# Four adaLN vectors move from TensorE to VectorE, and the later query projections are spread over six heads

## The chip, the cores and the metric

The kernel runs on one core of a Trainium2 chip. The metric is device time in microseconds (us) for one execution. The engines are PE (TensorE, matrix products; PEld is its weight load), DVE (VectorE), ACT (ScalarE), POOL (GpSimd) and SP (the queue that issues all DMA loads here). Each engine works through its own queue in order; a semaphore wait at the head of a queue holds everything behind it.

## The reference, cut to what matters

Two layers of a diffusion trunk over 512 latent tokens of width 1024, with 256 context tokens. Each layer begins with `adaln_params`: six vectors (shift, scale and gate, twice) that come from one condition vector.

```python
def adaln_params(cond, w, bias):
    m = jax.nn.silu(cond) @ w + bias            # w: 1024 x 6144, one row vector at a time
    return jnp.split(m[..., None, :], N_MOD, axis=-1)
...
sh1, sc1, g1, sh2, sc2, g2 = adaln_params(c, mod_w[i], mod_b[i])
h = modulate(rms_norm(x, norm_g[i, 0]), sh1, sc1)
y = attention_mixers(h, ...)  or  fourier_mix(h) @ w_f
x = x + g1 * rms_norm(y, norm_g[i, 1])
h = modulate(rms_norm(x, norm_g[i, 2]), sh2, sc2)
x = x + g2 * rms_norm(conv_ffn(h, ...), norm_g[i, 3])
```

Layer 0 mixes with attention: eight heads of 128, four global (A, heads 0 to 3, all 768 keys, rms norm on q and k) and four with a window (B, heads 4 to 7, the context and up to three blocks of 128 keys). Layer 1 mixes with a Fourier transform. What matters here are the vectors of layer 0 number 2 to 5: g1, sh2, sc2 and g2. Each is a product of a vector of 1024 with a 1024 x 1024 matrix of 4 MB. None of them is needed before the output projection's norm, right after attention; number 5 is first needed at the end of the first FFN.

## The kernel before, in words

All values are fp32. A product is done as three products of fp32r parts (`mm3`, lines 90 to 92): high x high, high x low, low x high. `split` (line 113) makes the parts: ACT casts the high part, DVE (or POOL) subtracts it for the low part. Weights come as 1 MB pieces into a ring of three buffers named `raw` (line 122); SP issues the loads in the order in which they are written, and a load waits until the buffer three loads earlier has been read. So a slow reader of one piece holds up the pieces behind it.

The order on each engine follows the order in which the code is written, moved about by the framework's scheduler from its own estimate of when operands are ready; the code steers it with generators that are advanced (`pump`) by a number of steps at given places.

Up to the attention heads the stages are:

- The start (line 47 on): shift and scale of layer 0 are made by channel tile on PE (`M0` to `M7`, function `mod_tile`, tiles `misc`, `modc`, `derc`), the inputs are modulated (`md_t`, `hh`, `hl`), and keys and values of two groups are accumulated.
- The early projections: groups `kb`, `vb`, `qa`, eight blocks of 48 products of 256 columns into `mm`. Their weights are loads `in_w_in`. Between them DVE and POOL do norm and rotation of keys and queries (`roped`, tiles `K`, `yT`, `sq`, `kst`, `qst`).
- The heads: for each head and each of four query blocks, scores `S` on PE, maximum on DVE (line 854), exponential on ACT, sum and reciprocal on DVE, scaling of `P` on POOL (line 870). One head later `pv` transposes `P` (`PT`, line 786), splits it (`th`, `tl`) and multiplies it with the values into `O`.
- The remaining query projections (heads 2 to 7: six blocks of 48 products into `gm`) are the generator `rest`, with eight steps for a block: ten steps before head 0 and the others beside heads 0 to 3, as the table `FILL` says, two entries for a query block.
- The four late vectors of layer 0 are the generator `gem0` (`gemv_pe`): sixteen pieces `in_mod_p` of 1 MB, four small products each (line 405), advanced by `FILL` beside heads 4 to 7; then eight transposes (line 412).
- The output projection's first tiles (`out_first`, 24 products of 512 columns twice and 24 of 256, into `gm` and `S`) beside the last head. Results of the first heads are kept in the queries' place (`kept`) and split into `hh`, `hl` when the projections are done with them.

The six vectors of layer 1 are made in the first FFN by `gemv_jobs`: for a vector, four pieces `in_mod_r`; of each, DVE multiplies two 128 x 1024 tiles by a column of the condition and adds them to a sum `gacc` (lines 376 and 379); then PE sums over partitions (line 384), ACT copies, PE transposes twice (line 390), DVE adds the bias. The FFN advances it 35 steps; a vector takes five.

Of the kernel before, what the change touches and what calls it, by code (L numbers as in the profile page):

```python
# [10 lines left out]
F32 = mybir.dt.float32  # L11
# [4 lines left out]
ALU = mybir.AluOpType  # L16
# [18 lines left out]
# what is traced where: how far work of one kind runs ahead of another kind's  # L35
# [6 lines left out]
# products that keep the PE's clock up: at the start, before the first sums' use, before the second FFN  # L42
# [3 lines left out]
# the start, in the order in which the loads arrive: M, shift and scale of a channel tile; W, its key and value  # L46
# weights; F, its products with a half of the latents or the context; X, B, R, what the norms need
START = ("M0 W0 X0 M1 B0 W1 F00 X1 F10 M2 W2 M3 F01 F11 F20 W3 F21 M4 R2 F30 F31 F02 W4 F12 F22 F32 M5 W5 F40 "
         "F41 M6 F42 W6 F50 F52 W7 F60 M7 F62 F51 F61 F70 F71 F72")
# how much of other work goes with each half block of a head's tokens  # L50
FILL = [[1, 0, 1, 2, 3, 2, 1, 2],
# [7 lines left out]

# columns of the packed parameter array  # L60
C_C, C_CC, C_MB, C_NG, C_CW, C_CB = 0, 8, 16, 112, 176, 440
C_SINK, C_ALL = 528, 532
# columns of the packed constants
# [4 lines left out]
def kernel(ctx: ExitStack, tc: tile.TileContext, a):  # L68
# [25 lines left out]
    # issued after another one on the same engine  # L94
# [4 lines left out]
    # work that must not be issued ahead of the last instruction traced before a fence on its engine  # L99
# [61 lines left out]
    # products that keep the PE's clock up where it would have to wait  # L161
# [4 lines left out]
    # sums over channels: four column tiles of the PE hold a quarter of the tokens each  # L166
# [5 lines left out]
    # 1 / sqrt(sum / D + eps)  # L172
# [10 lines left out]
    # the same where only the time until the end counts: sums on all partitions at once  # L183
# [14 lines left out]
    # one quarter of the tokens per quadrant of partitions: side by side, then to all partitions  # L198
# [12 lines left out]
    # h = x * am * R + bm for several channel tiles, shared out over the engines  # L211
# [15 lines left out]
    # squares of y: summed over channel tiles by GpSimd, the last one by the PE  # L227
    class YStat:
# [8 lines left out]
        def add(self, pps, src, hs):  # L237
# [9 lines left out]
            # the halves of the last one share a tile where they come one after the other  # L247
# [26 lines left out]
    # x += gate * rms_norm(y) for one channel tile  # L274
# [11 lines left out]
    # x += gate * rms_norm(y); then the next sub-layer's modulated input  # L286
# [20 lines left out]
    # the same, but what follows gets the input x * am only: the token's factor is applied after the products  # L307
    # over channels, and the shift is added there
    class Plain:
        # sums of squares go where the first and the last tile of y are done with  # L310
# [32 lines left out]
        # the factors: tokens on partitions, or on all partitions  # L343
# [23 lines left out]
    # adaLN off the critical path: products and sums on DVE, the sum over partitions on the PE  # L367
    def gemv_jobs(jobs, pps):
        for l, v in jobs:
            acc = mk(cp, [P, D], F32, "gacc", 1)  # L370
            for kk in range(4):
                w = raw([P, 2, D], a["mod_r"][v, kk])
# [25 lines left out]
    # the same on the PE: four column tiles take a quarter of the columns each  # L398
    def gemv_pe(pps):
        for j in range(2):  # L400
            ps = mk(pps, [P, T], F32, "gm", 1)
            for k in range(KC):
                w = raw([P, 2048], a["mod_p"][j, k])
                for q in range(4):
                    PE.matmul(ps[32 * q:32 * q + 32, :], lhsT=spad[:, k, :], rhs=w[:, q * T:(q + 1) * T],  # L405
                              start=k == 0, stop=k == KC - 1)
                yield
            rs = mk(cp, [P, T], F32, "sq", 2)
            S.copy(out=rs, in_=ps)
            tp = mk(pps, [P, T], F32, "gm", 1)  # L410
            for b in range(4):
                PE.transpose(out=tp[:, b * P:(b + 1) * P], in_=rs[:, b * P:(b + 1) * P], identity=ident)
            V.tensor_tensor(out=mods[:, 0, 2 * j + 2:2 * j + 4, :].rearrange("p v k -> p (v k)").rearrange(
                                "p (j b) -> p j b", b=4),
                            in0=tp.rearrange("p (b j r) -> p j b r", b=4, r=32)[:, :, :, 0],
                            in1=cols[:, C_MB + 16 * j + 16:C_MB + 16 * j + 32].rearrange("p (j b) -> p j b", b=4),
                            op=ALU.add)
            for v in (2 * j + 2, 2 * j + 3):
                derive(0, v)
            yield  # L420

# [4 lines left out]
    # output projection's weights for two channel tiles  # L426
    def out_weights(u, xp):
        r = raw([P, KC, 256], a["w_out"][u])
        ws = []
        for i in range(2):  # L430
            wh, wl = (xp.pair if u >= 2 else wpair)([P, KC, P])
            split(wh, wl, r[:, :, i * P:(i + 1) * P])
            ws.append([(wh[:, k, :], wl[:, k, :]) for k in range(KC)])
        return ws

        # ------------------------------------------------------------ attention
    with ExitStack() as es:
        ap = es.enter_context(tc.tile_pool(name="ap", bufs=1, reuse_waits="tile"))
        Q = yT.rearrange("p a b -> p (a b)").rearrange("p (t d) -> p t d", d=D)
# [302 lines left out]
        with ExitStack() as e2:  # L742
# [79 lines left out]
            for head in range(8):  # L822
# [64 lines left out]
                if head == 3:  # L887
                    pump(rest, 1000)
# [547 lines left out]
```

## Time and profile before

| | us |
|---|---|
| runs: median (lowest to highest of 3) | 1177.17 (1176.93 to 1181.68) |
| span of the profiled execution | 1176.5 |
| PE busy | 1134.0 (96%) |
| DVE busy | 751.6 (64%) |
| ACT busy | 512.2 (44%) |
| POOL busy | 201.1 (17%) |
| read from HBM | 141.98 MB |

The page gives no time of its own for the profiled execution beside its span; the span lies 0.7 us below the median of the runs. Stages by the span's clock: the start to 74 us, early projections to 120 us, heads to about 262 us, the rest of head 7 with the first output products to 279 us, output projection to about 340 us, first FFN to about 685 us, then the Fourier mixer and the second FFN. Busy times are shares of a span with very different stages; a stage has to be read by itself. PE's matmul records overlap, so that "busy" there means that no gap lies between records.

### The profile page before, as it was taken

Reading aid. Unit: us, or ns where it says so; the run is one execution under the profiler, and the core shown is the slowest. Engines: PE = TensorE matmul, PEld = TensorE weight load, DVE = VectorE, ACT = ScalarE, POOL = GpSimd, SP = SyncE. Lnnn points to the kernel's source line nnn. Section 1 sums busy time; section 2 is a strip of 40 time slices with the busy share of each in tenths; the row PEclk is TensorE's granted clock in tenths of the full one; section 3 lists DMA queues with packets and bytes.
Section 4 is the critical chain, followed back from the end, with each engine's and each line's share of the span. In section 5 each row is a group of like instructions: output and inputs, shape, how many; then the busy total and the mean of one; then the engine's idle time right before and its main releaser. Section 6 shows DMA issues by size and latency. Waiting matters only on the chain.

```text
span 1176.5 us, 17135 instructions
## 1 busy us (share of the span) xinstructions
PE 1134.0 (96%) x6878; PEld 946.1 (80%) x6878; DVE 751.6 (64%) x1215; ACT 512.2 (44%) x887; POOL 201.1 (17%) x213
## 2 busy tenths in 40 slices
PE   7999999999999999999999998988999999999995
PEld 4689898679898877777878998877788888888895
DVE  4673777675779685756665568988966532255555
ACT  3332356566554434322444445646644332234342
POOL 1132534222320000000000153663000000000013
PEclk9999999999999999999999999998999999999998
DMA  9432110874115353666622301621233222332112
GB/s 371 187 127 72 37 36 7 298 306 152 65 43 209 108 208 110 237 238 225 233 90 56 116 11 35 210 81 60 72 108 103 73 84 99 108 108 72 54 55 72
DMA packets 27127, 145.18 MB, mean 123 GB/s; under 512 B 2724, under 2 KB 7460, under 8 KB 14120
## 3 DMA queue, kind: packets, MB, share of 16 engines
q1 hardware_dynamic: 27048, 144.09, 35.0%
q8 instruction: 54, 0.88, 0.3%
q14 instruction: 25, 0.20, 0.1%
HBM read 141.98 MB, written 2.10 MB: 122 GB/s over the span
## 4 chain that ended last, share of the span: by engine, by line
PE 84%; DVE 11%; DMA 1%; ACT 1%; issue 1%; POOL 1%; SPq 0%; DVEq 0%; ACTq 0%; POOLq 0%
PE mm L90 24%; PE mm L92 23%; PE mm L91 23%; DVE md_t L278 2%; PE PT L786 2%; PE gm L405 1%; DVE hl L333 1%; PE O L90 1%; DVE wl L113 1%; DVE xT L280 1%; PE S L90 1%; PE O L91 1%; PE O L92 1%; PE S L92 1%; DMA xT<-in_xT 1%
## 5 line engine op out<-in xcount | busy, mean ns | idle before, releaser
L113 DVE TENSOR_TENSOR wl<-raw,wh 128x1024 fp32r<-128x1024 f32 (+1 forms) x139 | 167.6, 1210 | 207.8 <-ACT wh L113 207.5
L90 PE MATMUL mm<-hh,wh 128*128 128x512 f32 (+2 forms) x728 | 276.1, 379 | 0.0
L92 PE MATMUL mm<-hh,wl 128*128 128x512 f32 (+2 forms) x728 | 275.7, 379 | 0.0
L91 PE MATMUL mm<-hl,wh 128*128 128x512 f32 (+2 forms) x728 | 275.4, 378 | 0.0
L113 ACT CAST wh<-raw 128x1024 fp32r<-128x1024 f32 (+2 forms) x151 | 149.6, 999 | 183.4 <-PE mm L91 141.9
L90 PEld LDWEIGHTS mm<-hh,wh 128*128 128x128 f32 x728 | 137.7, 189 | 29.3 <-issue 1.2
L92 PEld LDWEIGHTS mm<-hh,wl 128*128 128x128 f32 x728 | 137.7, 189 | 27.9
L91 PEld LDWEIGHTS mm<-hl,wh 128*128 128x128 f32 x728 | 137.8, 189 | 27.5
L253 POOL TENSOR_TENSOR gacc<-gacc,sq 128x256 f32<-128x256 f32 (+1 forms) x35 | 31.5, 900 | 681.3 <-ACT sq L251 680.5
L90 PE MATMUL mm<-xh,wh 128*128 128x512 f32 (+1 forms) x368 | 131.5, 357 | 0.0
L91 PE MATMUL mm<-xl,wh 128*128 128x512 f32 (+1 forms) x368 | 130.6, 355 | 0.0
L92 PE MATMUL mm<-xh,wl 128*128 128x512 f32 (+1 forms) x368 | 130.5, 355 | 0.0
L90 PEld LDWEIGHTS mm<-xh,wh 128*128 128x128 f32 x368 | 69.2, 188 | 12.4 <-issue 1.2
L91 PEld LDWEIGHTS mm<-xl,wh 128*128 128x128 f32 x368 | 69.1, 188 | 11.1
L92 PEld LDWEIGHTS mm<-xh,wl 128*128 128x128 f32 x368 | 69.0, 187 | 11.0
L113 ACT CAST xh<-cv 128x512 fp32r<-128x512 f32 x44 | 27.3, 620 | 100.9 <-DVE cv L1008 100.9
L995 DVE SCALAR_TENSOR_TENSOR cv<-mm,cols,cv 128x511 f32<-128x511 f32 x83 | 61.8, 745 | 11.4 <-ACT cv L994 11.4
L994 ACT ACTIVATE cv<-mm,cols 128x512 f32<-128x512 f32 x83 | 64.2, 774 | 10.4 <-PE mm L92 10.4
L997 DVE SCALAR_TENSOR_TENSOR cv<-mm,cols,cv 128x511 f32<-128x511 f32 x83 | 62.2, 749 | 2.2
L1007 ACT ACTIVATE cv<-cv 128x512 f32<-128x512 f32 x44 | 27.8, 631 | 71.2 <-DVE cv L997 68.7
L379 DVE SCALAR_TENSOR_TENSOR gacc<-raw,scol,gacc 128x1024 f32<-128x1024 f32 x42 | 53.8, 1281 | 4.5 <-DMA raw<-in_mod_r 4.1
L91 PE MATMUL mm<-hl,xh 128*128 128x256 f32 (+1 forms) x160 | 47.3, 296 | 3.6 <-DVE hl L333 2.8
(358 smaller groups left out, 2238.7 us busy)
## 6 DMA issues: line engine op xcount, KB each, us to landing
raw<-in_w_up SPq DMA_DIRECT2D x44, 1024.0 KB, 5.0
raw<-in_mod_r SPq DMA_DIRECT2D x24, 1024.0 KB, 5.0
raw<-in_mod_p SPq DMA_DIRECT2D x16, 1024.0 KB, 6.4
raw<-in_w_down SPq DMA_DIRECT2D x16, 896.0 KB, 4.6
raw<-in_w_down SPq DMA_DIRECT2D x16, 512.0 KB, 3.7
raw<-in_w_in SPq DMA_DIRECT2D x6, 1024.0 KB, 5.0
raw<-in_w_out SPq DMA_DIRECT2D x4, 1024.0 KB, 6.0
raw<-in_w_f SPq DMA_DIRECT2D x8, 512.0 KB, 4.4
```

The costliest lines, as they stand in the source:

```text
L90: i = PE.matmul(out, lhsT=ah, rhs=bh, start=start, stop=False)
L91: PE.matmul(out, lhsT=ah, rhs=bl, start=False, stop=False)
L92: return i, PE.matmul(out, lhsT=al, rhs=bh, start=False, stop=stop)
L113: i = S.copy(out=h, in_=src), eng.tensor_tensor(out=l, in0=src, in1=f(h), op=ALU.subtract)
L253: G.tensor_tensor(out=self.acc[:, sl], in0=self.acc[:, sl], in1=sq[:, sl], op=ALU.add)
L278: m = V.scalar_tensor_tensor(out=t, in0=yT[:, k, hs], scalar=der[:, l, gi, k:k + 1], in1=R, op0=ALU.mult, op1=ALU.mult)
L379: held(V.scalar_tensor_tensor(out=acc, in0=w[:, i, :], scalar=scol[:, 0, k:k + 1], in1=acc, op0=ALU.mult, op1=ALU.add))
L786: PE.transpose(out=pt[:, j * P:(j + 1) * P], in_=Ps[j][:, off:off + P], identity=ident)
L994: S.activation(out=cv, in_=ps, func=AF.Identity, bias=bc, scale=wc[1])
L995: V.scalar_tensor_tensor(out=cv[:, 1:], in0=ps[:, :T - 1], scalar=wc[0], in1=cv[:, 1:], op0=ALU.mult, op1=ALU.add)
L997: V.scalar_tensor_tensor(out=cv[:, :T - 1], in0=ps[:, 1:], scalar=wc[2], in1=cv[:, :T - 1], op0=ALU.mult, op1=ALU.add)
L1007: S.activation(out=cg, in_=cg, func=AF.Silu)
```

## The change

`gemv_pe` and its pieces `in_mod_p` go. Vectors 2, 3 and 4 of layer 0 are now jobs of `gemv_jobs` beside the early projections, with a sum tile `pacc` of one buffer; two steps go with each of the eight blocks. Vector 5 becomes the first job of the first FFN, ahead of layer 1's six. `FILL` now holds ones and noughts for heads 0 to 5, all of it for the query projections; heads 6 and 7 have no entry. Five heads instead of three are kept, and are split in heads 6 and 7.

```diff
-FILL = [[1, 0, 1, 2, 3, 2, 1, 2], [2, 0, 1, 0, 1, 0, 2, 2], [3, 1, 3, 0, 0, 0, 1, 2], [2, 1, 1, 0, 0, 1, 1, 2],
...
+FILL = [[1, 0, 1, 1, 1, 1, 1, 1], [1, 0, 1, 1, 1, 1, 1, 1], [1, 1, 1, 1, 1, 1, 1, 1], [1, 0, 1, 0, 1, 0, 1, 0],
...
+KEPT = 5
-    def gemv_jobs(jobs, pps):
+    def gemv_jobs(jobs, pps, pool=None):
         for l, v in jobs:
-            acc = mk(cp, [P, D], F32, "gacc", 1)
+            acc = mk(pool or cp, [P, D], F32, "pacc" if pool else "gacc", 1)
             for kk in range(4):
-                w = raw([P, 2, D], a["mod_r"][v, kk])
+                w = raw([P, 2, D], a["mod_r"][6 * l + v - 2, kk])
...
-    def gemv_pe(pps):
...
+            gem0 = gemv_jobs([(0, v) for v in (2, 3, 4)], pps, pj)
             for g, kind in enumerate(["kb", "vb", "qa"]):
...
-                    pump(project(ps, ws, sh, sl, t0), 100)
+                    pr = project(ps, ws, sh, sl, t0)
+                    for _ in range(2):
+                        pump(pr, 4)
+                        pump(gem0)
...
-                if head < 3:
+                if head < KEPT:
                     S.copy(out=kept(head)[0], in_=po.rearrange("p (t d) -> p t d", d=P))
...
-                        pump(rest if is_a else gem0, FILL[head][2 * j + i])
-                    if head == 4 and j < 3:
-                        src, (dh, dl) = kept(j)
+                        pump(rest, FILL[head][2 * j + i] if head < 6 else 0)
+                    i = 4 * (head - 6) + j
+                    if 0 <= i < KEPT:
+                        src, (dh, dl) = kept(i)
                         split(dh, dl, src, G)
-                if head == 3:
+                if head == 5:
                     pump(rest, 1000)
...
-            pump(pend)
-            pump(gem0, 1000)
-            pump(pend)
+            pump(pend, 2)
...
-                 gemv_jobs([(1, v) for v in range(6)], pps))
+                 gemv_jobs([(0, 5)] + [(1, v) for v in range(6)], pps))
```

What this does to three queues. On SP, before, from the first projection weights on (a name's number tells one buffer use from another; `in_w_in` are projection weights, `gqk` and `mask` small constants, `in_mod_p` pieces of the four vectors for PE):

```order
L122 DMA raw_838<-in_w_in 128x2048
L122 DMA raw_1006<-in_w_in 128x2048
L122 DMA raw_1166<-in_w_in 128x2048
L122 DMA raw_1176<-in_w_in 128x2048
L613 DMA Rs_751<-in_gqk 128x256
L615 DMA md_t_753<-in_mask 128x256
L122 DMA raw_1524<-in_w_in 128x2048
L122 DMA raw_1850<-in_w_in 128x2048
L122 DMA raw_2263<-in_mod_p 128x2048
```

And now, with `in_mod_r`, the pieces that DVE sums:

```order
L122 DMA raw_838<-in_w_in 128x2048
L122 DMA raw_874<-in_mod_r 128x2048
L122 DMA raw_902<-in_mod_r 128x2048
L122 DMA raw_936<-in_mod_r 128x2048
L122 DMA raw_964<-in_mod_r 128x2048
L589 DMA Rs_751<-in_gqk 128x256
L591 DMA md_t_753<-in_mask 128x256
L122 DMA raw_1035<-in_mod_r 128x2048
L122 DMA raw_1040<-in_w_in 128x2048
L122 DMA raw_1075<-in_mod_r 128x2048
L122 DMA raw_1103<-in_mod_r 128x2048
L122 DMA raw_1133<-in_mod_r 128x2048
```

Between the first and the second group of projection weights there now stand five pieces for the vectors, and so on to the third group.

On DVE at the last channel tile of the start (`M7`; `modc` and `derc` are its shift and scale, `md_t` the modulated input of which PE's last start products wait), before:

```order
L113 TENSOR_TENSOR wl_845<-raw_838,wh_844 128x1024
L223 SCALAR_TENSOR_TENSOR hl_67<-md_t_710,modc_154,hh_66 128x256
L542 TENSOR_REDUCE modc_154<-misc_674 128x4
L544 TENSOR_TENSOR modc_154<-modc_154,cols_61 128x4
L546 TENSOR_SCALAR derc_155<-modc_154,cols_61 128x2
L221 SCALAR_TENSOR_TENSOR md_t_720<-xT_64,derc_155,Rs_231 128x256
```

And now:

```order
L113 TENSOR_TENSOR wl_845<-raw_838,wh_844 128x1024
L223 SCALAR_TENSOR_TENSOR hl_67<-md_t_710,modc_154,hh_66 128x256
L376 TENSOR_SCALAR pacc_873<-raw_874,scol_74 128x1024
L518 TENSOR_REDUCE modc_154<-misc_674 128x4
L379 SCALAR_TENSOR_TENSOR pacc_873<-raw_874,scol_74,pacc_873 128x1024
L520 TENSOR_TENSOR modc_154<-modc_154,cols_61 128x4
L379 SCALAR_TENSOR_TENSOR pacc_873<-raw_902,scol_74,pacc_873 128x1024
L522 TENSOR_SCALAR derc_155<-modc_154,cols_61 128x2
L379 SCALAR_TENSOR_TENSOR pacc_873<-raw_902,scol_74,pacc_873 128x1024
L221 SCALAR_TENSOR_TENSOR md_t_720<-xT_64,derc_155,Rs_231 128x256
```

Four sums of the first vector have come between the tile's products and its modulated input.

On PE in head 7, near its last scores (`S_2939` before, `S_2910` now), before:

```order
L786 MATMUL PT_2913<-con_63,P_2748 128x128
L405 MATMUL gm_2605<-raw_2920,spad_151 32x512 x4
L90 MATMUL O_2807<-th_2878,wh_2493 128x384
L91 MATMUL O_2807<-tl_2879,wh_2493 128x384
L92 MATMUL O_2807<-th_2878,wl_2494 128x384
L90 MATMUL S_2939<-kh_87,qh_2764 128x256
L91 MATMUL S_2939<-kl_88,qh_2764 128x256
L412 MATMUL gm_2928<-con_63,sq_2926 128x128 x4
```

And now:

```order
L765 MATMUL PT_2900<-con_63,P_2749 128x128
L90 MATMUL O_2798<-th_2865,wh_2512 128x384
L827 MATMUL S_2910<-kh_87,ql_2766 128x256
L830 LDWEIGHTS identb_82
L830 MATMUL S_2910<-maskb_81,identb_82 128x128
L90 MATMUL S_2932<-hh_66,wh_2893 128x512
L91 MATMUL S_2932<-hl_67,wh_2893 128x512
L91 MATMUL O_2798<-tl_2866,wh_2512 128x384
```

The adaLN products (line 405) and their transposes are gone from between the head's own instructions; single products of the output projection (`S_2932<-hh`) have been drawn forward to there.

More of the change, by code (lines that the diff above doesn't have):

```diff
@@ L49 @@
          "F41 M6 F42 W6 F50 F52 W7 F60 M7 F62 F51 F61 F70 F71 F72")
-FILL = [[1, 0, 1, 2, 3, 2, 1, 2],
[4 rows of a table removed]
+FILL = [[1, 0, 1, 1, 1, 1, 1, 1],
[2 rows of a table added]
         [1, 0, 1, 0, 1, 0, 1, 0],
[2 rows of a table removed]
[2 rows of a table added]
+KEPT = 5
 C_C, C_CC, C_MB, C_NG, C_CW, C_CB = 0, 8, 16, 112, 176, 440
@@ L395, in gemv_jobs @@
             derive(l, v)
-            yield
-    def gemv_pe(pps):
[L400 to L419, printed above, removed]
             yield
@@ L747 @@
             S0 = [mk(aps, [P, 1024], F32, "S", 2)]
-            gem0 = gemv_pe(aps)
             rest = queries(aps, w_q)
@@ L1401, in _layout @@
     mod_s = mw[0, :, :, 0:2].transpose(3, 1, 0, 2, 4).reshape(KC, P, KC, 256)
-    mod_p = i['mod_w'][0].reshape(KC, P, 3, 2048)[:, :, 1:].transpose(2, 0, 1, 3)
     mr = i["mod_w"].reshape(2, 4, 2, P, 6, D).transpose(0, 4, 1, 3, 2, 5).reshape(12, 4, P, 2, D)
@@ L1414, in _layout @@
     xT = chan(i["x"][0]).reshape(P, KC, 2, HT).transpose(0, 2, 1, 3)
-    out.update(cols=cols, gqk=np.concatenate(rep[1:], 1), xT=xT, cT=chan(i["ctx"][0]), mod_s=mod_s, mod_r=mr[6:], mod_p=mod_p, w_kva=kva, w_in=np.stack(wi),
+    out.update(cols=cols, gqk=np.concatenate(rep[1:], 1), xT=xT, cT=chan(i["ctx"][0]), mod_s=mod_s, mod_r=mr[2:], w_kva=kva, w_in=np.stack(wi),
                w_out=w_out, w_up=w_up, w_f=w_f, w_ny=wf[:, P])
```

10 rows, old and new, of the table FILL are left out of this document.

## The prediction

> **What bounds the kernel now.** I read the page's first part, then the chain by line, then stretches of the span, since the change touches three stages with different limits: early projections (to 120 us), heads (to 279 us) and first FFN.
>
> ```profile
> PE 1134.0 (96%) x6878; PEld 946.1 (80%) x6878; DVE 751.6 (64%) x1215; ACT 512.2 (44%) x887; POOL 201.1 (17%) x213
> by line: PE mm L90 23.5%; PE mm L92 23.3%; PE mm L91 23.3%; DVE md_t L278 2.1%; PE PT L786 1.5%; PE gm L405 1.4%; issue 1.1%; DVE hl L333 1.1%; PE O L90 1.0%; DVE wl L113 1.0%; DVE xT L280 0.9%; PE S L90 0.9%; PE O L91 0.9%; PE O L92 0.8%;
> ```
>
> PE is the bound over the whole; line 405, which the change removes, holds 1.4% of the chain, 16.5 us of 1176.5. The stages are less alike:
>
> ```profile
> core 0: us, PE busy (x) PEld busy (x) DVE busy (x) ACT busy (x) POOL busy (x), PEclk, DMA share, GB/s
> 64.00:130.00 66.00, 64.58 (x507) 61.19 (x506) 36.17 (x78) 19.48 (x36) 23.64 (x32) 1.00 0.20 68
> 120.00:130.00 10.00, 8.58 (x67) 7.80 (x66) 9.29 (x20) 2.94 (x5) 4.77 (x4) 1.00 0.00 1
> 130.00:140.00 10.00, 9.90 (x72) 9.55 (x70) 6.49 (x13) 5.53 (x9) 4.54 (x5) 1.00 0.01 2
> 140.00:150.00 10.00, 8.21 (x62) 7.59 (x62) 9.66 (x26) 3.69 (x8) 4.82 (x5) 1.00 0.31 105
> 202.00:220.00 18.00, 18.00 (x131) 11.27 (x130) 12.16 (x27) 8.44 (x21) 5.53 (x6) 1.00 0.73 247
> 235.00:249.00 14.00, 14.00 (x106) 9.02 (x104) 9.35 (x24) 7.71 (x20) 2.81 (x4) 1.00 0.78 284
> 249.00:262.00 13.00, 13.00 (x91) 9.81 (x90) 11.14 (x28) 10.39 (x23) 2.75 (x4) 1.00 0.81 322
> 380.00:460.00 80.00, 80.00 (x349) 63.76 (x348) 55.02 (x65) 33.43 (x45) 0.00 (x0) 1.00 0.42 145
> ```
>
> Beside the early projections (64 to 130 us) DVE is idle for 29.8 us. At the first heads PE has gaps already: 1.4, 0.1 and 1.8 us, 3.3 in 30 us, with DVE busy 9.3 and 9.7 of 10. In the heads that carry the four vectors, and in the FFN, PE has no gap.
>
> **What leaves PE.** Sixteen pieces of four products, and eight transposes.
>
> ```profile
> 202.88 1.92 PE L405 MATMUL gm<-raw,spad 128*32 128x512 f32 x16
> 204.73 0.50 PE L90 MATMUL O<-th,wh 128*128 128x512 f32 x1
> 249.94 1.06 PE L405 MATMUL gm<-raw,spad 128*32 128x512 f32 x8
> 228.11 0.60 PE L412 MATMUL gm<-con,sq 128*128 128x128 f32 x4
> ```
>
> The first row is two pieces; the next product starts 1.85 us later, so a piece takes at least 0.93 us, sixteen 14.8. The chain's 16.5 counts the seams as well; I take that, with 0.9 for the transposes (two sets of four; the row reads 0.60, their ends overlap): -17.4 us, if PE has other work at once.
>
> **What DVE gets early.** Three vectors, each eight 128 x 1024 products.
>
> ```profile
> L379 DVE SCALAR_TENSOR_TENSOR gacc<-raw,scol,gacc 128x1024 f32<-128x1024 f32 x42 | 53.8, 1281 | 4.5 <-DMA raw<-in_mod_r 4.1
> L376 DVE TENSOR_SCALAR gacc<-raw,scol 128x1024 f32<-128x1024 f32 x6 | 4.5, 752 | 19.7 <-PE misc L384 19.7
> L384 PE MATMUL misc<-gacc,ones 128*32 128x256 f32 x48 | 3.8, 391 | 0.0
> raw<-in_mod_r SPq DMA_DIRECT2D x24, 1024.0 KB, 5.0
> raw<-in_w_in SPq DMA_DIRECT2D x6, 1024.0 KB, 5.0
> ```
>
> A vector is 0.752 + 7 x 1.281 = 9.72 us, three 29.2, with small adds 30. The stretch had 29.8 idle: DVE becomes full there, and whatever it waits for becomes delay. Three places matter. First, the last channel tile of the start:
>
> ```profile
> 66.70 0.17 DVE L542 TENSOR_REDUCE modc<-misc 128x4 f32<-128x16 f32 x1 [0.76 <-PE misc L540]
> 67.38 0.88 DVE L221 SCALAR_TENSOR_TENSOR md_t<-xT,derc,Rs 128x256 f32<-128x256 f32 x2
> 69.92 0.40 PE L90 MATMUL mm<-wh,hh 128*128 128x512 f32 x1
> ```
>
> In the new order two of the sum's instructions stand between `modc` and `derc`, ahead of tile 7's `md_t`. `md_t` ended at 68.26 and PE's first product on the tile began at 69.92, about 1.5 us of slack after the split; two products of 1.28 and the wait for their piece move `md_t` to about 71, and PE, which has nothing else here, stands for some 2.4 us. Second, SP's queue: twelve loads `in_mod_r` now stand among the six `in_w_in`, in the ring of three. A projection weight is issued only when DVE has read the piece three back. With 1.28 us an instruction, two to a piece, the second group's weight goes out near 76.7 and lands 5.0 later, 81.7; its split follows on a busy DVE, and PE stands about 1.7 us, later 0.7 again. Third, DVE's own queue behind that: normalisation of the last query blocks and the first head's maximum come behind the last sums.
>
> ```profile
> 132.46 0.96 DVE L854 TENSOR_REDUCE mx<-S 128x1 f32<-128x768 f32 x1 [1.06 <-PE S L92]
> 156.49 0.95 DVE L854 TENSOR_REDUCE mx<-S 128x1 f32<-128x768 f32 x1
> L632 DVE TENSOR_REDUCE qst<-sq 128x4 f32<-128x512 f32 x2 | 1.3, 674 | 0.0
> L113 DVE TENSOR_TENSOR wl<-raw,wh 128x1024 fp32r<-128x1024 f32 x1 | 1.2, 1216 | 0.0
> ```
>
> Summing DVE's instructions in the new order with these durations, the first maximum (132.46) comes near 139.9, 7.4 later: 4.8 of PE's stalls and 2.6 of DVE's backlog. Bounds: all 30 us of sums fit the idle 29.8 (delay 0.3), or half of that idle time was waiting that stays waiting (15). I take the walk's 7.4, midway. The heads then give some back: with query steps moved out of heads 0 to 3, a block's normalisation (two passes of 0.67) and a weight split of 1.22 leave DVE between the two maxima, 2.6 us, so that at 156.49 I count 7.4 - 2.6, about +5.
>
> A rule of the Trainium skill speaks against the change here. The row first:
>
> ```profile
> 77.97 1.91 POOL L637 TENSOR_TENSOR sq<-sq,gacc 128x128 f32<-128x128 f32 x2 [0.93 <-DVE kst L632]
> 81.62 0.93 POOL L637 TENSOR_TENSOR sq<-sq,gacc 128x128 f32<-128x128 f32 x2 [0.93 <-DVE kst L632]
> 78.07 1.48 DVE L113 TENSOR_TENSOR wl<-raw,wh 128x1024 fp32r<-128x1024 f32 x1
> ```
>
> The same POOL work takes 1.91 beside DVE's two-operand split and 0.93 alone, about 1 us more. The twelve pairs of sums will run beside POOL's rotation of the same eight blocks. If a rotation in three stands on the path, the delay grows by 3 us, to +8; this is a rival below, the sum goes without it, since POOL is idle for 42 of the 66 us. The Trainium skill ("SBUF — State Buffer", section "SBUF: two separate sides") says that a DVE instruction with two SBUF inputs and a GpSimd instruction that reads SBUF exclude each other for the whole instruction; by these rows the trace agrees.
>
> **Query steps moved.** 48 steps in all as before.
>
> ```profile
> 161.45 0.28 PE L90 MATMUL gm<-wh,hh 128*128 128x256 f32 x1
> 161.81 0.28 PE L90 MATMUL gm<-wh,hh 128*128 128x256 f32 x1
> ```
>
> Three products in 0.36 us, so a step of six is 0.72. Heads 0 to 3 lose 12 steps, 8.6 us; heads 4 and 5 get 13. Counted from head 1's third score on, about six steps come in: +4.4 us of PE work. PE work from there to the end of the first output products: -17.4 + 4.4 = -13.0.
>
> **Heads 6 and 7 without fill.** Here sums and query steps are both gone. What a row block needs between its scores and its use:
>
> ```profile
> 239.53 0.82 DVE L854 TENSOR_REDUCE mx<-S 128x1 f32<-128x640 f32 x1 [0.19 <-PE S L851]
> 242.56 0.80 POOL L870 TENSOR_SCALAR P<-P,mx 128x640 f32<-128x640 f32 x1 [3.69 <-PE PT L786]
> L113 POOL TENSOR_TENSOR hl<-yT,hh 128x512 fp32r<-128x512 f32 x3 | 3.8, 1289 | 1.1 <-ACT hh L113 1.1
> L802 ACT COPY yT<-O 128x512 f32<-128x512 f32 x3 | 1.8, 596 | 0.0
> 413.20 0.64 PE L384 MATMUL misc<-gacc,ones 128*32 128x256 f32 x8
> ```
>
> 3.83 us from maximum to scaled `P`. PE's own work of such a head: 235:249 and 249:262 are about a head each, 14 and 13 us, with four pieces of 0.93 in each, which leaves 10.3 and 9.3, a mean of 9.8, or 2.45 a block. If every block waited, 8 x 1.4 = 11 us, and some 3 more at head 7's last values: upper bound 14; lower 0, since `pv` runs one head behind and the output projection's first products (24 of 512 columns, the scheduler draws some 18 of all forward) can stand in. The nearest row is 120:150, heads with little fill: 11% gaps, over 35 us 4. These heads have none at all, and five kept results are now split there, the subtraction for some of them on POOL (1.29 us each) in front of its scalings, up to four in a row: 4 + 4 x 1.29 would be 9; I take 8, since not all of them meet a scaling that is due.
>
> **The rest.** Vector 5 in the FFN: 10 us on DVE, which is busy 55 of 80 there (69%), so hidden while that holds; its PE tail costs eight sums and two transposes, 0.6 + 0.3 = +0.9 with PE full. Without the cover it would cost 10. SP loads the same 16 MB; 12 MB move to 64:130, where DMA was 20% busy (+12 MB at 5.0 us a piece fit), and leave 202:262 at 73 to 81%; nothing waited for DMA in PE's row there, so no gain. Two more heads are copied into the kept place on ACT at 0.60 each, in place of a split: ACT has idle time there (10.4 of 13 us at most), so 0, and 1.2 if ACT were late.
>
> Sum on the span: +5 early, -13.0, +8, +0.9 = +0.9: 1177.4. The span is 0.7 below the median of the runs, so 1178.
>
> **Rivals.**
> (1) The early jam is worse: PE finds no work while loads wait for DVE and DVE for loads. Each sum pair of 2.56 us must meet a landed piece; if the ring of three leaves DVE idle for a tenth of the 66 us (6.6) on top and the sum tile's one buffer a transpose tail (about 0.9 a vector, 2.7), the early delay is +15 to 16, and the time 1188. It decides from an early delay of some +10 on. For: DVE is full; against: loads are spread at two per block.
> (2) The sums on PE were only fill. In heads 4 to 7 the row chain, not PE, would be the limit, taking `in_mod_p` out frees nothing and stalls replace it: stalls 16 instead of 8, 1186. For: 120:150 shows gaps where fill was thin; against: 202:262 shows none.
> (3) The early cover holds: the 29.8 idle us take the sums, +3 early, and stalls 2, as the output products cover the end: 3 - 13.0 + 2 + 0.9 = -7.1, 1170.
> (4) The port costs 3 us more: 1181, still no change.
> (5) The change doesn't do what it says: the scheduler moves the sums behind the first maximum. The new order shows them ahead of it; under 1 in 50.
>
> By the Trainium skill ("TensorE: Matmul & The Clock Gate", section "What's actually happening") the clock halves after one idle window of about 3.4 us. PE's 3.3 us of gaps in 120:150 came in pieces and the granted clock stayed 1.00; the stalls forecast (2.4 at most in one) are shorter, so nothing is added.
>
> **How the numbers follow.** About 0.5%, 5.9 us, is what a measurement of this kernel can tell from no change: faster is below 1171.3, slower above 1183. Forecast (1178, with its own spread of 1172 to 1183) 0.40; (4) 0.10; (1) 0.20; (2) 0.12; (3) 0.18. Faster 0.18, same 0.50, slower 0.32. The range runs from below (3) to (1), 1168 to 1188; half of (1) and a part of (3) lie outside, about 2 in 10.
>
> **What would show it.** Line 405 gone from the chain; DVE near 100% in 66 to 125 us; `md_t` of tile 7 near 71; the first maximum near 140 and the one of 156.49 near 161; PE without gaps in heads 4 and 5; gaps of 6 to 10 us in heads 6 and 7, ended by POOL's scaling; the FFN's length within 1 us. Wrong if the first maximum comes at 148 (rival 1), if heads 6 and 7 show over 14 us of gaps (2), or if the early stage ends within 3 us of before (3).

## The result, and the profile after

The changed kernel takes 1185.15 us (median of 14 runs, 1181.27 to 1187.13) beside 1179.39 us for the kernel before (14 runs on the same chips, 1176.24 to 1183.32). The ratio is 1.0042, with a 95% interval from 1.0027 to 1.0057, which is 0.42% or 5.0 us slower (the two medians are 5.8 apart). That is inside "within 0.5%", and 7 us above the point forecast of 1178; 2.2 of these 7 are the kernel before itself, whose median was 1177.17 in the three runs that the forecast started from. The profiled execution has a span of 1182.1 us, 5.6 more than before.

First the page's first part and the chain by line, after:

```profile
PE 1127.8 (95%) x6782; PEld 947.9 (80%) x6782; DVE 788.9 (67%) x1247; ACT 513.4 (43%) x891; POOL 212.8 (18%) x215
by line: PE mm L90 22.3%; PE mm L92 22.0%; PE mm L91 22.0%; DVE md_t L278 2.1%; issue 2.0%; PE PT L765 1.3%; DVE hl L333 1.1%; DMA raw<-in_w_in 1.0%; DVE wl L113 1.0%; DVE xT L280 0.9%; DMA raw<-in_mod_r 0.9%; POOL sq L613 0.8%; PE O L90 0.
```

Line 405 has left the chain, as the change says. In its place stand two transfers into the ring, weights (`in_w_in`, 1.0%) and pieces for the early sums (`in_mod_r`, 0.9%), 22 us together, and POOL's rotation (line 613). None of the three stands in the chain's lines shown of before. The stretches (columns as before: busy us of each engine, granted clock, share of DMA, GB/s):

```profile
64.00:130.00 66.00, 59.03 (x456) 54.40 (x455) 54.71 (x84) 17.04 (x32) 27.39 (x28) 1.00 0.69 246
66.00:125.00 59.00, 53.16 (x415) 49.73 (x414) 47.81 (x76) 15.88 (x30) 26.14 (x26) 1.00 0.68 250
130.00:140.00 10.00, 8.38 (x58) 8.32 (x58) 8.04 (x20) 2.43 (x5) 5.50 (x5) 0.83 0.22 89
150.00:165.00 15.00, 11.35 (x67) 10.07 (x66) 12.94 (x33) 7.60 (x14) 7.39 (x7) 0.89 0.20 71
202.00:220.00 18.00, 17.89 (x125) 15.74 (x124) 12.85 (x27) 9.74 (x21) 4.23 (x5) 1.00 0.00 1
235.00:249.00 14.00, 11.99 (x77) 9.69 (x77) 12.00 (x26) 7.55 (x18) 6.79 (x7) 1.00 0.23 76
249.00:262.00 13.00, 11.66 (x82) 9.91 (x81) 11.06 (x29) 9.05 (x22) 4.68 (x5) 1.00 0.01 3
380.00:460.00 80.00, 80.00 (x349) 63.74 (x348) 57.75 (x70) 33.11 (x44) 0.00 (x0) 1.00 0.45 156
```

Beside the early projections PE lost 5.6 us of 66 (59.03 busy, 64.58 before). DVE is at 54.71, not at 66, and from 66 to 125 us, where the prediction expected it near 100%, at 47.81 of 59, 81%: it waits too. Two stretches have a lowered clock. The later heads have gaps of 2.0 and 1.3 us where there were none, and the FFN is as full as it was. PE's waits of over 0.45 us up to the first maximum, the first maximum itself (a row of DVE), and the longest waits of PE in the heads (start, length, instruction, in brackets the idle time before it and what ended it):

```profile
70.06 0.50 PE L90 MATMUL mm<-wh,hh 128*128 128x512 f32 x1 [1.62 <-ACT hh L222]
92.95 0.44 PE L390 MATMUL misc<-con,sq 128*128 128x128 f32 x2 [2.89 <-ACT sq L387]
114.85 0.39 PE L91 MATMUL mm<-wl,hh 128*128 128x256 f32 x1 [0.71 <-DVE wl L113]
117.18 0.39 PE L91 MATMUL mm<-wl,hh 128*128 128x256 f32 x1 [0.63 <-DVE wl L113]
128.13 0.64 PE L384 MATMUL misc<-pacc,ones 128*32 128x256 f32 x8 [0.81 <-DVE pacc L379]
131.62 0.44 PE L390 MATMUL misc<-con,sq 128*128 128x128 f32 x2 [1.95 <-ACT sq L387]
143.77 0.96 DVE L833 TENSOR_REDUCE mx<-S 128x1 f32<-128x768 f32 x1 [1.10 <-PE S L92]
158.89 0.44 PE L765 MATMUL PT<-con,P 128*128 128x128 f32 x2 [2.77 <-POOL P L849]
243.18 0.33 PE L765 MATMUL PT<-con,P 128*128 128x128 f32 x1 [1.24 <-POOL P L849]
258.56 0.44 PE L765 MATMUL PT<-con,P 128*128 128x128 f32 x2 [1.34 <-POOL P L849]
```

The two largest early waits are not those at tile 7 or at a weight. They stand at the vectors' own tails, at the transposes (390) that follow a sum over partitions (384), both in PE's queue in the midst of the projections.

To compare kernels I count from one event that all of them have, the sum `modc` of tile 7 (66.70 before, 65.05 after; over all kernels below it lies between 64.4 and 69.0), to the first maximum, and to the first `md_t` of the output projection's norm (line 278). In every kernel it starts 0.5 us after PE begins that tile's transposes. The rows, before and after (the one of 166.61 is the seventh maximum, the one at 156.49 before):

```profile
299.43 0.88 DVE L278 SCALAR_TENSOR_TENSOR md_t<-yT,der,Rs 128x256 f32<-128x256 f32 x2
```

```profile
65.05 0.17 DVE L518 TENSOR_REDUCE modc<-misc 128x4 f32<-128x16 f32 x1
166.61 0.95 DVE L833 TENSOR_REDUCE mx<-S 128x1 f32<-128x768 f32 x1
302.35 0.88 DVE L278 SCALAR_TENSOR_TENSOR md_t<-yT,der,Rs 128x256 f32<-128x256 f32 x2
```

| kernel | to first maximum | to output norm | ratio of times to before (95%) |
|---|---|---|---|
| before | 65.8 | 232.7 | 1 |
| changed | 78.7 | 237.3 | 1.0042 (1.0027 to 1.0057) |
| own tile for the copy | 79.8 | 239.9 | 1.0058 (1.0037 to 1.0080) |
| changed, no early vectors | 65.8 | 223.2 | 0.9935 (0.9920 to 0.9950) |
| before, no late vectors | 65.8 | 219.3 | 0.9893 (0.9873 to 0.9913) |
| before, vector 5 in the FFN | 65.8 | 233.4 | 1.0027 (1.0014 to 1.0039) |
| own places for the pieces | 81.0 | 239.7 | 1.0061 (1.0037 to 1.0085) |
| sums without loads (a third in the start) | 69.3 | 227.8 | 0.9976 (0.9962 to 0.9990) |
| loads with short sums | 71.3 | 230.0 | 0.9966 (0.9951 to 0.9981) |
| changed, no vector 5 | 79.1 | 237.6 | 1.0029 (1.0011 to 1.0047) |
| late tails, own places | 84.6 | 242.9 | 1.0096 (1.0073 to 1.0119) |
| late tails | 85.0 | 243.5 | 1.0079 (1.0053 to 1.0105) |
| changed, old query order | 79.1 | 232.4 | 0.9996 (0.9977 to 1.0015) |
| two early vectors | 71.2 | 228.5 | 0.9950 (0.9934 to 0.9966) |

So the changed kernel is 13.0 us late at the first maximum and 4.6 late at the output norm: the heads gave back 8.4. With 0.6 more in the first FFN (below) that makes 5.2, which fits the 5.0 of the ratio. The spans' 5.6 are made otherwise: 1.7 less before tile 7 and 2.1 more behind the first FFN, stretches in which the change adds or removes no work. Over the traces here these two differ by up to 4.5 and 3.1 us, so a single span is no measure of a change of this size.

### The profile page after: what moved, and what is told of

Read it like the earlier page. It is cut to its first block, busy times and chain, and to the rows that moved or that the text cites. A ratio compares the mean times of both kernels' runs of the same rounds, so it can differ in the third digit from the quotient of the medians.

```text
span 1182.1 us, 16996 instructions
## 1 busy us (share of the span) xinstructions
PE 1127.8 (95%) x6782; PEld 947.9 (80%) x6782; DVE 788.9 (67%) x1247; ACT 513.4 (43%) x891; POOL 212.8 (18%) x215
## 4 chain that ended last, share of the span: by engine, by line
PE 79%; DVE 12%; POOL 2%; DMA 2%; ACT 2%; issue 2%; DVEq 0%; SPq 0%; ACTq 0%; POOLq 0%
PE mm L90 22%; PE mm L92 22%; PE mm L91 22%; DVE md_t L278 2%; PE PT L765 1%; DVE hl L333 1%; DMA raw<-in_w_in 1%; DVE wl L113 1%; DVE xT L280 1%; DMA raw<-in_mod_r 1%; POOL sq L613 1%; PE O L90 1%; DVE pacc L379 1%; PE O L91 1%; PE gm L90 1%
## 5 line engine op out<-in xcount | busy, mean ns | idle before, releaser
L90 PEld LDWEIGHTS mm<-xh,wh 128*128 128x128 f32 x368 | 69.2, 188 | 12.6 <-issue 1.6
L91 PEld LDWEIGHTS mm<-xl,wh 128*128 128x128 f32 x368 | 69.3, 188 | 10.9
L379 DVE SCALAR_TENSOR_TENSOR gacc<-raw,scol,gacc 128x1024 f32<-128x1024 f32 x49 | 62.7, 1280 | 6.8 <-DMA raw<-in_mod_r 6.1
```

The costliest lines, as they stand in the source:

```text
L90: i = PE.matmul(out, lhsT=ah, rhs=bh, start=start, stop=False)
L91: PE.matmul(out, lhsT=ah, rhs=bl, start=False, stop=False)
L379: held(V.scalar_tensor_tensor(out=acc, in0=w[:, i, :], scalar=scol[:, 0, k:k + 1], in1=acc, op0=ALU.mult, op1=ALU.add))
```

## The experiments

**Is it the tail's shared tile?** The wait of 2.89 us ends with ACT's copy, which had waited for POOL to leave `sq`:

```profile
92.52 0.37 ACT L387 COPY sq<-misc 128x256 f32<-128x256 f32 x1 [4.55 <-POOL K L619]
```

```diff
-            rs = mk(cp, [P, T], F32, "sq", 2)
+            rs = mk(pool, [P, 256], F32, "psq", 1) if pool else mk(cp, [P, T], F32, "sq", 2)
```

> The changed kernel, with one edit: the ACT copy of each early vector (L387) goes to a tile of its own instead of the two `sq` tiles that the rotation of keys and queries uses. Theory A (the early delay is mostly the vectors' own tails: PE stands before the transposes L390 for 2.89 and 1.95 us because the copy waits for POOL to finish with `sq`): the two gaps fall under 0.5 us, the granted clock of 130 to 140 us goes back to 1.00, the first maximum comes near 138 instead of 143.8, and the time falls by 4 to 6 us, to about 1179. Theory B (DVE is full beside the projections and sets the delay, the gaps on PE are only where it shows): other gaps take their place, the first maximum stays within 1 us and so does the time, about 1184.

Ratio 1.0058; the first maximum came 1.1 us later than in the changed kernel. The two waits are gone and others stand there:

```profile
107.62 0.64 PE L384 MATMUL misc<-pacc,ones 128*32 128x256 f32 x8 [2.10 <-DVE pacc L379]
138.80 0.88 PE L795 MATMUL PT<-con,yT 128*128 128x128 f32 x6 [2.54 <-POOL yT L619]
```

PE now waits for the sum itself, and later for the queries' rotation, which comes behind the sums on DVE. Theory A falls as far as the shared tile goes: the wait was where the delay showed, not what made it. The tails themselves still stand in PE's queue here.

**What do the early vectors cost?**

```diff
-            gem0 = gemv_jobs([(0, v) for v in (2, 3, 4)], pps, pj)
+            gem0 = gemv_none((2, 3, 4))      # mods = bias, then derive
```

> The changed kernel without the products of vectors 2, 3 and 4 of layer 0 (their bias alone is used). It prices the early sums with their loads and tails. Theories A and B: the first maximum comes near 132.5 as before the change, and the time falls by the whole early cost, 8 to 11 us, to 1174 to 1177. Theory C (the heads are bound by their row chain and swallow an early delay): the first maximum comes earlier all the same, but the time falls by 3 us or less, 1181 or more.

Ratio 0.9935, against 1.0042 with them: 1.07%, 12.6 us. The first maximum is back at 65.8 exactly, and the output norm comes 14.1 us earlier. The heads swallow nothing of an early delay. The expectation's 8 to 11 was low.

**What was line 405 worth?**

```diff
-            gem0 = gemv_pe(aps)
+            gem0 = gemv_none((2, 3, 4, 5))
```

> The kernel before without the products of the four late vectors of layer 0 (no `in_mod_p`, no L405; their bias alone is used). It prices what leaves PE. If PE sets the pace of heads 4 to 7 (theories A and B, and the prediction's term): 17.4 us less, about 1161. If the products were only fill in heads that the row chain paces (theory C): 5 us less or nothing, 1173 to 1178, with gaps on PE before the transposes of P in heads 4 to 7.

Ratio 0.9893, 12.6 us; the output norm comes 13.4 us earlier. Of the 17.4 us of PE work, 13.4 were on the path and 4.0 were fill. Waits that the products used to cover (a head's queries, then the scaled `P`):

```profile
227.95 0.39 PE L90 MATMUL S<-kh,qh 128*128 128x256 f32 x1 [1.10 <-ACT qh L113]
242.67 0.44 PE L792 MATMUL PT<-con,P 128*128 128x128 f32 x2 [1.34 <-POOL P L876]
```

**One vector alone to the FFN.**

```diff
-                w = raw([P, 2048], a["mod_p"][j, k])
-                for q in range(4):
+                nq = 4 - 2 * j
+                w = raw([P, nq * T], a["mod_p"][j, k][:, :nq * T])
+                for q in range(nq):
...
-                 gemv_jobs([(1, v) for v in range(6)], pps))
+                 gemv_jobs([(0, 5)] + [(1, v) for v in range(6)], pps))
```

> The kernel before, with only vector 5 moved: it is the first job of the first FFN, and the second half of the PE pieces shrinks to two products of four (the later eight pieces are loaded at half size). FILL and all else as before. If PE sets the pace in heads 6 and 7: 16 products of 64 and half the bytes less, about 3.5 to 4.4 us less, and the FFN costs nothing or up to 0.9 us: 1174 to 1175. Theory C: no change, 1178 to 1180.

Ratio 1.0027: slower, where either theory had expected no loss. A miss, and the trace says why. A round of two products (four records, since each product leaves two) takes as long as the round of four did, whose eight records took 1.06 us in the row at 249.94 above:

```profile
242.14 1.05 PE L406 MATMUL gm<-raw,spad 128*32 128x512 f32 x4
```

All rounds together are 17.2 us of PE here and 17.3 before. So nothing left PE, and the FFN's cost came on top. The run says nothing about theory C. Of its 3.2 us, 0.7 lie ahead of the output norm and 1.2 from there to the norm after the first FFN. The rest is not settled; this execution was also 1.2 us longer behind the first FFN, where the edit touches nothing.

**Is it the ring of three?** The chain of the changed kernel has four landings between 98 and 130 us, the first two of which are:

```profile
98.19 5.32 DMA raw<-in_mod_r
106.26 6.20 DMA raw<-in_w_in
```

```diff
+                if pool:
+                    w = spare[kk % 2]            # the halves of yT
+                    SY.dma_start(out=w, in_=a["mod_r"][6 * l + v - 2, kk])
```

> The changed kernel with one edit: the twelve early pieces `in_mod_r` go into two places of their own (the two halves of `yT`, unused until the queries are written) instead of the ring of three that the projection weights use. Theory D (a projection weight is issued only when DVE has read a sum's piece three uses back, and then takes 5 to 6 us to land: four such landings, 22.5 us, stand in the chain of waits between 98 and 130 us): the loads leave the chain, the first maximum comes 6 to 9 us earlier than 143.8, and the time falls by as much, to 1176 to 1179. Theory B (DVE's 30 us of sums are the delay, wherever the pieces lie): 2 us or less, 1183 or more.

Ratio 1.0061, no gain. The waits at a weight's split are gone from PE, and these stand instead:

```profile
92.44 0.44 PE L395 MATMUL misc<-con,sq 128*128 128x128 f32 x2 [2.71 <-ACT sq L392]
108.01 2.61 DVE L384 SCALAR_TENSOR_TENSOR pacc<-yT,scol,pacc 128x1024 f32<-128x1024 f32 x2 [2.86 <-DMA yT<-in_mod_r]
110.77 0.94 PE L389 MATMUL misc<-pacc,ones 128*32 128x256 f32 x8 [2.51 <-DVE pacc L384]
```

DVE waits for a piece in its own place, and PE for DVE at the tail. The ring alone is not shown to be the cause either; but the run has put two places in its stead, which hold up the pieces themselves, so it doesn't clear the ring.

**DVE's work alone, and the loads alone.**

```diff
+                if pool:
+                    w = spare[kk % 2]            # early vectors: no load
+                else:
+                    w = raw([P, 2, D], a["mod_r"][6 * l + v - 2, kk])
```

> The changed kernel without the loads of the early vectors: their 24 sums read what lies in `yT`, so DVE's work, the tails and the order stay and no transfer is tied to them. (The three vectors are not the reference's.) It prices DVE's work alone. Theory D: of the early cost of 12 to 13 us some 4 remain, 1175 to 1177. Theory B: 10 or more remain, 1181 to 1184.

```diff
+                        n = 8 if pool else D
-                        held(V.scalar_tensor_tensor(out=acc, in0=w[:, i, :], ...
+                        held(V.scalar_tensor_tensor(out=acc[:, :n], in0=w[:, i, :n], ...
```

> The changed kernel with all twelve early loads through the shared ring, but DVE multiplies only 8 of 1024 columns after each vector's first product, so 21 of the 24 sums shrink to about 0.1 to 0.2 us each. (The three vectors are not the reference's.) It prices loads, ring and tails without DVE's work. Theory D: 6 us or more of the early cost remain, 1178 or more. Theory B: 3 or less remain, 1172 to 1175.

Sums without loads: the first maximum 3.5 us late, ratio 0.9976, 4.8 us above the kernel with no early vectors. Loads with 3 of the 24 sums at full size: 5.5 late, 0.9966, 3.7 us above it. By their numbers theory D's expectation holds for the first run (some 4 remain) and fails for the second (6 or more); theory B's fails for the first (10 or more) and is nearly met by the second (3 or less).

But the first run is not what its expectation says. The sums' share of the engines, before and behind 60 us:

```profile
0.00:60.00 60.00, 0.00 (x0) 0.00 (x0) 9.69 (x8) 0.91 0.72 279
60.00:140.00 80.00, 1.92 (x24) 0.47 (x24) 19.65 (x16) 1.00 0.21 70
```

With no load to wait for, the eight sums of the first vector ran in the start, and only sixteen, 19.65 us, beside the projections (the changed kernel has all 24 there, 29.60 us). So 3.5 us is the price of two vectors' sums with three tails, and no run prices all 30 us of sums without loads. In the second run the short sums take 8.1 us of DVE, more than expected (0.27 us each). What the two runs show is that about 20 us of sums without loads, or all loads with 8 us of sums, cost far less than the 13.0 at the first maximum and the 12.6 us of time that the whole costs.

**Vector 5 in the first FFN.**

```diff
+            pump(gemv_none((5,)))                                # vector 5: bias
...
-                 gemv_jobs([(0, 5)] + [(1, v) for v in range(6)], pps))
+                 gemv_jobs([(1, v) for v in range(6)], pps))
```

> The changed kernel without the products of vector 5 in the first FFN (its bias alone). The prediction's term is 0.9 us (its PE tail; DVE's 10 us hidden): 1184. If the vectors of layer 1, which now end at 658 us instead of 598, delay the stage behind the FFN as well, 2 to 3.5 us: 1181 to 1183.

Ratio 1.0029 beside 1.0042: 1.5 us, with intervals that overlap. The trace is sharper: from the output norm's first `md_t` to the one after the FFN are 388.2 us before, 388.0 here, 388.8 in the changed kernel. Over all traces, the eleven kernels with vector 5 there take 388.8 to 389.4 and the three without 388.0 to 388.2: it costs 0.6 to 1.4 there, with 0.9 forecast. Behind the FFN this kernel took no less than the changed one (491.5 and 490.9 us to the end), so the traces don't support the second expectation.

**Both couplings at once, and the tails alone.** Three sum tiles, two of them in `cT`; the pieces in `yT` (first run) or in the ring (second).

```diff
-            gem0 = gemv_jobs([(0, v) for v in (2, 3, 4)], pps, pj)
+            gem0 = gemv_early(jobs0, accs0, True)      # pieces only; second run: False, the ring
...
+            gemv_tail(jobs0, accs0, pps)               # after the last early block
```

> The changed kernel with two couplings taken away at once: the early pieces have two places of their own (as in the run with the own places), and the three vectors are summed into three tiles (two of them in `cT`, which is dead by then), so that their PE sums, ACT copies and transposes all stand after the last early projection instead of between the projections. Theory E (each coupling alone, the shared ring and the tails in PE's queue, suffices to hold PE, so removing one showed nothing): the early cost falls to what DVE's work alone costs (4.8 us in the run without loads), so 6 to 8 us less than the changed kernel, 1177 to 1180 beside a kernel before at 1180. Theory F (DVE's work and the loads together exceed the stage, in whatever order): 2 us or less.

> The changed kernel with the tails alone moved behind the last early projection (three sum tiles), the pieces still in the shared ring of three. Theory E: the ring still holds the weights, 2 us or less gained against the changed kernel. If the tails in PE's queue are the chief coupling: 5 us or more gained, though the own place for the copy alone gained nothing.

Ratios 1.0096 and 1.0079, the slowest of all. In the first the projections did flow: from tile 7 to the last product of the last early block were 55.7 us (53.8 before, 64.4 in the changed kernel). In the second they were 59.5, with waits of 2.11 and 0.81 us at weights' splits. So taking the tails out from between the projections frees 4.9 of the 10.6 us that PE had lost by then, and taking the pieces out of the ring as well 3.8 more (with three sum tiles DVE no longer waits for a tail either). Then, in the first, came the tails in a row:

```profile
135.86 0.69 PE L427 MATMUL misc<-con,sq 128*128 128x128 f32 x2 [11.21 <-ACT sq L424]
```

```profile
132.63 2.77 POOL L649 TENSOR_TENSOR sq<-sq,gacc 128x256 f32<-128x256 f32 x2 [1.46 <-DVE qst L644]
135.44 0.37 ACT L424 COPY sq<-misc 128x256 f32<-128x256 f32 x1 [4.05 <-DVE qtm L153]
```

The first tail's copy takes turns in `sq` with the last block's rotation and starts when that ends on POOL (135.40; the view names DVE's `qtm`, which ended at the same moment and which the copy doesn't read). The rotation is behind the sums on DVE. PE, with the transposes at the head of its queue, stood 11.2 us (7.9 in the second run). Of theory E it is shown that removing both couplings frees the projections; that each alone suffices to hold them is not, since the tails alone gave back about half. That the time would follow failed by my own placement of the tails.

**The order of the query projections.**

```diff
-KEPT = 5
+KEPT = 3
-                if head == 5:
+                if head == 3:
                     pump(rest, 1000)
-                    i = 4 * (head - 6) + j
+                    i = 4 * (head - 4) + j
```

with the rows of `FILL` for heads 0 to 3 as before and noughts behind.

> The changed kernel with the query projections as before the change (all beside heads 0 to 3, three kept results split in head 4, nothing beside heads 4 to 7); the early sums and vector 5 in the first FFN stay. If spreading over six heads costs time of itself (without vectors the kernel before reaches the output norm 4.0 us earlier than the changed one, 285.9 against 289.9, from the same first maximum): 3 to 5 us less than the changed kernel. If the spreading covers waits that the late start causes: no gain, or up to 3 us more.

Ratio 0.9996: 0.46%, 5.4 us less than the changed kernel; at the output norm 4.9 us earlier, though the first maximum is as late (79.1). Spreading the query projections, with the two more kept results that go with it, costs about 5 us of itself.

**A version from the findings.** Vectors 2 and 3 early, vector 4 on PE in heads 4 to 6 (four products of 256 columns a round), vector 5 in the FFN, the old query order, the copy in its own tile.

```diff
+EARLY0 = [[0, 1], [1, 1], [1, 1], [1, 1], [1, 0], [1, 0], [1, 0], [0, 0]]
...
-            gem0 = gemv_jobs([(0, v) for v in (2, 3, 4)], pps, pj)
+            gem0 = gemv_jobs([(0, v) for v in (2, 3)], pps, pj)
...
+                    PE.matmul(ps[32 * q:32 * q + 32, :256], lhsT=spad[:, k, :], rhs=w[:, i, q * 256:(q + 1) * 256], ...
-                        pump(rest, FILL[head][2 * j + i] if head < 6 else 0)
+                        pump(rest if is_a else gem4, FILL[head][2 * j + i])
```

> A version made from the findings: of the three early vectors two stay on DVE beside the projections (20 us of sums instead of 30, 8 loads instead of 12 in the ring, none beside the last block, ACT's copy in a tile of its own); vector 4 goes back to PE beside heads 4 to 6 as eight rounds of four products of 256 columns; vector 5 stays in the first FFN; the query projections stay beside heads 0 to 3 as before the change. If the early cost is an overload of the stage (sums alone 3.5 us and loads alone 5.5 us later at the first maximum, both together 13.0), two thirds of it fit far better: first maximum 3 to 6 us later than in the kernel before, counted from tile 7's sum, and the sum is -13.5 (PE vectors) + 4 (vector 4 on PE) + 4.5 + 1.5 (first FFN) = -3.5, a ratio of about 0.997 to the kernel before. If the cost is set by the order (any early sums ahead of the weights), two vectors cost 8 to 9 us and the ratio is 1.000 to 1.002.

Ratio 0.9950 (0.9934 to 0.9966): 1175.12 us beside 1181.12, faster than the kernel before and than the changed one. Before the first maximum only one wait of PE of over 0.4 us is left that the kernel before has not, the one at tile 7, and vector 4's eight rounds are 4.9 us busy, 0.61 a round:

```profile
71.62 0.49 PE L87 MATMUL mm<-wh,hh 128*128 128x512 f32 x1 [1.61 <-ACT hh L219]
L402 PE MATMUL gm<-raw,spad 128*32 128x256 f32 x64 | 4.9, 385 | 0.0
```

The first maximum is 5.4 us late, inside the 3 to 6 expected; two vectors do not cost two thirds of 13, which would be 8.7. The output norm comes 4.2 us earlier than before and the FFN costs 0.8 more, together -3.5, as the expected sum said; by the ratio it is -5.9 us (-4.0 to -7.8), and the difference is not explained. The version changes four things of the changed kernel at once; only the old query order (about 5 us) and the copy's tile (no gain) were run by themselves.

## Why the forecast landed where it did

The forecast of no measurable change held, with luck: the early term was 9.1 us too small and the heads' two terms together 4.5 too large, so that half of the first error was cancelled by the second. With the early error alone the sum would have been +10, and the time outside the 0.5%.

- **Early delay: the step that failed.** The walk over DVE's order gave 7.4 us at the first maximum and +5 in the sum. It was 13.0, and 14.1 at the output norm against the kernel without early vectors. Two premises of the walk were wrong. It took DVE as full, and DVE was at 81% (66 to 125 us), since it waited itself, for pieces and for PE. And it left out the vectors' tails on PE: 0.9 us was charged for one in the FFN, and nothing for three here. Where PE stood can be added up: the tails are 2.5 us of work (by the starts of the products around them) and 2.89 + 0.81 + 1.95 us of standing, 8.2 us; tile 7 is 1.6 (2.4 forecast), the third weight group 1.3 (0.71 + 0.63; forecast were 1.7 at the second, where no wait came, and 0.7 later), the lowered clock 1.5 (last section); less 0.8, since of two waits of before ahead of the first maximum (0.47 and 0.71) only 0.43 is left. That is 8.2 + 1.6 + 1.3 + 1.5 - 0.8 = 11.8 of the 13.0. It says where, not why: with the copy's waits taken away PE stood elsewhere, and with the tails taken out the projections won 4.9 us. Nor did the heads give back 2.6 by the seventh maximum (156.49 before): it came 11.8 us late, not 5.
- **Heads.** -13.0 and +8 in the sum, -5. Measured with the early part taken away: 223.2 - 232.7 = -9.5, made of -13.4 (line 405, of which I had taken all 17.4 as path) and +3.9 for the spread and what goes with it (223.2 against 219.3). For the spread I had put 4.4 of moved steps and 8 of stalls; the gaps behind `P` were there (1.24, 1.34), but from 235 to 262 us PE had 3.3 us of gaps in all, and the run with the old order prices the whole at 4.9. The two terms were too large by about 8 us, line 405's too large by 4, and so the heads came out 4.5 us better than forecast.
- **First FFN.** +0.9 forecast, 0.6 to 1.4 measured, with DVE at 57.75 of 80 and PE full: the cover held.
- **Rivals.** Rival 1 had the early stage nearly right in size (15 to 16; 13 to 14 came) and was wrong in its end, since the heads gave more back. Its mechanism, the ring and the sum tile's tail, is borne out in part: own places gained nothing, but with the tails moved the ring cost the projections 3.8 us, and the changed kernel's DVE waits 1.7 us for a tail before the third vector. Rival 2 holds for 4.0 of 17.4 us. Rival 3 is out. Rival 4 is real on POOL: the rotation's 128-column product went from 620 ns to 1024 (rows of before and after, 64 to 140 us), and the keys' scaling from 538 to 987, but no run here isolates what of it is on the path. In the version with two early vectors the two are as slow (1148 and 974) with the first maximum only 5.4 late, which speaks against its being most of the 13.0.

```profile
L637 POOL TENSOR_TENSOR sq<-sq,gacc 128x128 f32<-128x128 f32 x8 | 4.8, 620 | 19.9 <-DVE maskb L616 17.1 <-DVE kst L632 2.8
```

```profile
L613 POOL TENSOR_TENSOR sq<-sq,gacc 128x128 f32<-128x128 f32 x8 | 8.0, 1024 | 22.5 <-ACT V L632 19.7 <-DVE kst L608 2.8
```

What stays open: why the early cost rises so steeply. About 20 us of sums beside the projections cost 3.5 us without loads and 5.4 with eight loads, 30 us with twelve loads 13.0, and the run that was to price the 30 us alone had a third of them in the start. The four attempts to remove one coupling or two (own copy, own places, late tails, both) each put another wait in its place. The runs show that no single one of them is the whole cause, and that with a third less of both loads, and the copy in its own tile, more than half of the cost is gone; they don't show a single mechanism.

## What to carry to other kernels

Work put into an engine's idle time must be counted with all that it queues on the other engines: here PE, full before, stood 5.7 us in all at the tails of two vectors, each a microsecond of work, because they were in the midst of its queue and waited for late producers. Idle time in a stage is not all usable: filling all of it (30 us into 29.8) cost 13 at the first maximum, two thirds of it 5.4. A run that leaves a part out to price the rest must be looked at in the trace as well: without its loads a third of the work went to another stage. And taking work off the bounding engine should be priced by leaving it out on the chip first: it was 13.4 us where the profile's rows had been read as 17.4.

## What the runs showed of the hardware that I had not expected

**Products side by side.** With stationary operands (the loaded side of a product) of 32 columns on four column tiles, two products of 512 columns took 1.05 us and four took 1.06. A narrower moving operand does shorten a round: 0.61 us at 256 columns (4.9 over eight rounds) against 1.08 at 512 (17.3 over sixteen).

**The clock falls after shorter pauses than I took for safe, and not each time.** The prediction had added nothing for the clock. After the waits of 0.81 and 1.95 us the products' spacing went from 0.12 to 0.21 us for some 16 products, 1.5 us lost:

```profile
132.45 0.41 PE L91 MATMUL gm<-wl,hh 128*128 128x256 f32 x1
132.66 0.41 PE L92 MATMUL gm<-wh,hl 128*128 128x256 f32 x1
...
136.03 0.29 PE L91 MATMUL gm<-wl,hh 128*128 128x256 f32 x1
136.15 0.28 PE L92 MATMUL gm<-wh,hl 128*128 128x256 f32 x1
```

The wait of 2.77 us at 158.89 was followed by the lower clock as well (0.89 in its stretch), and so was the same wait in the runs with sums alone (2.76 us, 0.69 in the 5.5 us from its end) and loads alone (2.73, 0.69). In the kernel without early vectors it was not; its stretch, and the wait:

```profile
140.00:155.00 15.00, 11.38 (x71) 9.77 (x72) 13.53 (x33) 7.11 (x15) 7.39 (x7) 1.00 0.19 71
```

```profile
147.59 0.44 PE L771 MATMUL PT<-con,P 128*128 128x128 f32 x2 [2.76 <-POOL P L855]
```

So whether a wait of this length costs clock depends on more than its length. The Trainium skill ("TensorE: Matmul & The Clock Gate", section "What's actually happening") says that the window of about 3.4 us is free-running; a dependence on where the wait falls agrees with that, but that a pause of under 3 us can lower the clock at all is this case's measurement, against my reading of the Trainium skill.
